# A quarter of the second pass's raw weights loaded early, no loads in ScalarE's queue, and the last rotations in another order

## The chip, the cores and the metric

The kernel runs on one core of a Trainium2 chip. A core has TensorE (PE in the profile; its weight loads are PEld), VectorE (DVE), ScalarE (ACT), GpSimd (POOL) and SyncE (SP), and 16 DMA engines that move data between HBM and the core. SP, ACT and POOL can issue transfers; the profile writes SPq, ACTq and POOLq for that. Each engine works through its own list of instructions in order and waits for others by semaphores. The metric is the device time of one execution in microseconds (us); a kernel's time is the median of its runs.

## The reference, cut to what matters

One decoder layer on x of 4096 tokens by 1024, in float32: an RMSNorm, one projection into eight parts, dilated softmax attention (8 heads of 64, three branches), retention (4 heads, key width 64, value width 128) in chunks of 128 tokens, SiLU gates, an output projection, the residual and a last RMSNorm.

```python
h = rms_norm(x, norm_gain[layer])
proj = h @ w_in
qa, ka, va, ga, qr, kr, vr, gr = jnp.split(proj, cuts, axis=-1)
attn = merge_heads(dilated_attention(split_heads(qa, 8), split_heads(ka, 8), split_heads(va, 8)))
ret = merge_heads(retention(split_heads(qr, 4), split_heads(kr, 4), split_heads(vr, 4)))
mixed = jnp.concatenate([jax.nn.silu(ga) * attn, jax.nn.silu(gr) * ret * ret_gn_gain], axis=-1)
x = x + mixed @ w_out
return rms_norm(x, final_gain)
```

q and k of attention are rotated by position in halves of 32, q and k of retention in pairs. All of the output is needed to float32 precision.

## The kernel before

**Products.** Each float32 factor is split in a high part, rounded on ACT to the type that PE takes (fp32r), and a low part, the difference, on DVE or POOL; a product is three matmuls (hi hi, hi lo, lo hi).

**Phase 1** (function `phase1`) makes q, k, v and the retention's q and k from `w1`, in two passes over the tokens: pass 0 makes k of attention and v, pass 1 q of attention and q and k of retention. Each pass has 8 blocks of 512 tokens. A block is done by a scheme with seven products of half the size (P1, P5, P6, P3, P7, P2, P4, in this order) instead of eight; each product takes two steps (one for each bank of output columns), so a block has 14 steps (`STEPS`) of 48/2 = 24 matmuls. The products' right sides are quarters of the weights (A and B are the two halves of the raw rows of `w1`; rows 0 to 511 are "a", rows 512 to 1023 "b") or sums of them: D = A - B of "a" on POOL, S1, S2 and S4 on DVE. Each is split before use, and all splits together need more room than there is: `HOMES` names, for each product and pass, the tiles that its hi and lo parts lie in, and `ROOM` what tiles these are (most belong to phase 2: wh, w0 to w7, q00 to q11, hr, hc, kk; p40 and p41 are phase 1's own). So at the change of passes the raw weights of pass 1 (4 MB) come into tiles that pass 0 has done with, are scaled, summed and split there, and the splits go into tiles that later products of pass 0 free: P1 of pass 1 goes to kk, which P3 of pass 0 holds up to its last matmul.

**The order** is written by hand. The loop at the end of `phase1` goes through the steps; `at(step, fn, ...)` lists what is issued behind a step's matmuls, with front=True ahead of what is listed already. `s = STEPS * NBLK` is the first step of pass 1 and `STEPS * NB2` the end of the phase. A step says where an instruction stands in its engine's list, not when it runs. For block q, `hi_x` and `lo_x` split x (tile h), `snapshot` (ACT) and `join` (DVE) carry sums over between PSUM banks (tile m), `values` (ACT) and `store_values` write v, `rotate` (DVE, six operations on 128x512) turns q and k, `hi_o`/`lo_o` split what was turned (tile hl) and `store_o`, `store_r` store it. For the norm, tokens are loaded as rows into the tiles "xn" and "tabR" (`load_n`) and squared on ACT (`square`); pass 1 uses "tabR" for the rotation's tables and "xn" for parts of P4's weights, loaded a second time (`split_p4`, tile `raw`).

**Phase 2** is attention and retention. Its instructions are built from two generators: `attention` (score products S into two PSUM banks, row maximum on DVE, exponential P on ACT, transposes T, products with v) and `filler` (chunk after chunk of 128 tokens: values V of retention with weights `w2`, in 8 steps k, with `scores` Rs, `decayed_q` qg, `decayed_k` kd, `outputs` Ro, `next_state`, of the chunk before). Filler runs alone up to `LEAD`, and then as the slots of attention allow. Each chunk's x is loaded as hr (one tile) and split into hc (three tiles). Its first loads are issued in phase 1 (`first_k`, `first_q`, `first_chunk`) or at its start (`first_loads`): the constants and the mask on SP, and the rest of head 0's q (columns 512 to 2047) and k (from 1024) by ACT. **Phase 3** makes the gates and the output projection.

## Time and profile before

| what | value |
|---|---|
| runs | 2404.93, 2403.29, 2402.48 us, median 2403.29 |
| profiled execution | 2404.88 us, span 2403.1 us |
| PE busy | 2276.7 us, 95% of the span |
| DVE, ACT, POOL busy | 1736.7, 1140.5, 785.3 us |
| DMA | 405.07 MB, mean 169 GB/s |
| granted TensorE clock, mean | 0.98 |

The span is the time from the first to the last instruction of the profiled execution; the execution's own time lies 1.8 us above it. Times of rows are in us from the span's start. The page cuts the span in 40 slices of 60 us and gives the busy share of each in tenths:

```profile
PE   6999995999994999999999999998899999999998
```

PE is at 9 almost everywhere; the first slice, the seventh (360 to 420, the change of passes), the thirteenth (720 to 780, from phase 1 to phase 2) and two around 1700 (phase 2 to 3) lie below. A row of a timeline gives start, length, engine, line, operation, what it writes and reads, how often; in brackets stands how long the engine had been idle and what ended that.

### The profile page before, as it was taken

The numbers are of one execution on the slowest core, as the hardware profiler recorded it, in microseconds if no ns is written. First come the engines' busy times: TensorE is split into PE (matmuls) and PEld (weight loads), VectorE is DVE, ScalarE is ACT, GpSimd is POOL, SyncE is SP. The second block draws the span as 40 slices with busy tenths as digits, with TensorE's granted clock in tenths as the row PEclk, the third lists the DMA queues.
The fourth block names the chain that finished last, engine by engine and source line by source line (L and its number), as shares of the span: only waits on it lengthen the run. The fifth ranks groups of instructions, "written<-read, shape, count | busy, mean of one in ns | idle before, by whom it ended". The sixth has DMA issues, their size and how long they took to land. (4 is left out here: it accounts for less than half of the span.)

```text
span 2403.1 us, 47344 instructions
## 1 busy us (share of the span) xinstructions
PE 2276.7 (95%) x16808; PEld 2049.9 (85%) x16808; DVE 1736.7 (72%) x4231; ACT 1140.5 (47%) x3082; POOL 785.3 (33%) x961
## 2 busy tenths in 40 slices
PE   6999995999994999999999999998899999999998
PEld 5899995999993888888888888877789999999997
DVE  6776867998985878787887879786665655655654
ACT  5555554332331666767666666667322322322221
POOL 1343433222222545344543535456121121121110
PEclk8999998999997999999999999999999999999999
DMA  6678775555468565758585775746676665566653
GB/s 193 202 235 273 225 239 174 175 152 180 151 190 198 134 160 140 186 124 194 136 179 144 160 159 133 177 129 194 147 184 156 144 170 152 141 164 154 148 154 92
DMA packets 447789, 405.07 MB, mean 169 GB/s; under 512 B 210040, under 2 KB 397176, under 8 KB 442688
## 3 DMA queue, kind: packets, MB, share of 16 engines
q1 hardware_dynamic: 412112, 324.79, 52.9%
q0 software_dynamic: 29968, 57.07, 8.0%
q10 hardware_dynamic: 5472, 20.19, 2.6%
q8 instruction: 133, 2.18, 0.4%
q14 instruction: 104, 0.85, 0.1%
HBM read 283.12 MB, written 118.64 MB: 167 GB/s over the span
## 5 line engine op out<-in xcount | busy, mean ns | idle before, releaser
L1064 DVE CUSTOM_DVE_ANT_0 S<-S,mask 128x256 f32<-128x256 f32 (+1 forms) x768 | 308.6, 402 | 165.2 <-PE S L1043 127.3
L1071 ACT ACTIVATE P<-S,nm 128x256 f32<-128x256 f32 (+1 forms) x768 | 337.3, 449 | 46.5 <-DVE nm L1064 43.4
L50 PE MATMUL g<-h,wg 128*128 128x256 f32 x1024 | 289.4, 283 | 0.0
L323 ACT ACTIVATE h<-xt 128x1024 fp32r<-128x1024 f32 (+1 forms) x115 | 119.5, 1039 | 246.8 <-DVE xt L315 105.8
L1080 PE MATMUL T<-ident,P 128*128 128x128 f32 x1368 | 213.6, 274 | 0.0
L49 PE MATMUL po<-wo,m 128*128 128x512 f32 x512 | 200.8, 392 | 0.1
L1632 POOL TENSOR_TENSOR rs<-v,mhalf 128x1 f32<-128x1 f32 x32 | 17.5, 547 | 547.2 <-DVE v L1630 529.0
L50 PEld LDWEIGHTS g<-h,wg 128*128 128x128 f32 x1024 | 195.8, 191 | 0.0
L1113 PE MATMUL O<-pt,v 128*64 128x128 f32 (+1 forms) x1968 | 195.7, 325 | 0.0
L1043 PE MATMUL S<-kk,qc 128*128 128x256 f32 x1024 | 187.2, 306 | 7.0 <-issue 2.7
L48 PE MATMUL po<-wohi,m 128*128 128x512 f32 x448 | 178.7, 399 | 7.7 <-ACT m L40 6.6
L1043 PEld LDWEIGHTS S<-kk,qc 128*128 128x128 f32 x1024 | 149.8, 190 | 35.6 <-issue 17.1
L50 PE MATMUL po<-wohi,m 128*128 128x512 f32 x448 | 177.7, 397 | 0.2 <-DVE m L41 0.2
L811 POOL TENSOR_TENSOR hc<-hr,hc 128x512 fp32r<-128x512 f32 x64 | 86.4, 1351 | 266.8 <-ACT hc L810 196.5
L1113 PEld LDWEIGHTS O<-pt,v 128*64 128x64 f32 x1968 | 121.1, 137 | 60.4 <-issue 31.5
L1080 PEld LDWEIGHTS T<-ident,P 128*128 128x128 f32 x1368 | 164.1, 141 | 0.2 <-ACT wg0hi L87 0.2
L327 DVE TENSOR_TENSOR h<-xt,h 128x1024 fp32r<-128x1024 f32 (+1 forms) x115 | 137.8, 1198 | 36.5 <-ACT h L323 36.4
L1571 ACT ACTIVATE e<-g 128x256 f32<-128x256 f32 x128 | 48.3, 379 | 239.2 <-PE g L50 222.8
L40 ACT ACTIVATE m<-e 128x256 fp32r<-128x256 f32 x128 | 53.1, 417 | 227.8 <-DVE e L1578 133.7
L1071 ACT ACTIVATION_READ_ACCUMULATOR P<-S,nm 128x1 f32 x768 | 157.6, 205 | 0.0
L48 PE MATMUL g<-h,wg1hi 128*128 128x256 f32 x512 | 144.8, 284 | 2.3 <-ACT e L1571 2.3
L49 PE MATMUL g<-h,wg1hi 128*128 128x256 f32 x512 | 145.8, 285 | 1.1 <-DVE h L859 0.9
(278 smaller groups left out, 6519.2 us busy)
## 6 DMA issues: line engine op xcount, KB each, us to landing
hr<-in_xT_dram SPq DMA_DIRECT2D x61, 512.0 KB
xt<-in_xT_dram POOLq DMA_DIRECT2D x60, 512.0 KB, 9.1
q<-dr_q SPq DMA_DIRECT2D x120, 256.0 KB
v<-dr_v SPq DMA_DIRECT2D x96, 256.0 KB
wb<-dr_w SPq DMA_DIRECT2D x128, 192.0 KB
o<-dr_o SPq DMA_DIRECT2D x192, 128.0 KB
xn<-in_x_dram ACTq DMA_DIRECT2D x32, 512.0 KB
dr_v<-vo SPq DMA_DIRECT2D x64, 256.0 KB
```

Source lines behind the costliest of these rows:

```text
L40: nc.scalar.activation(dst[:, 0], src, AF.Copy)
L48: nc.tensor.matmul(out, wh, xh, start=first and i == 0, stop=False)
L49: nc.tensor.matmul(out, wh, xl, start=False, stop=False)
L50: nc.tensor.matmul(out, wl, xh, start=False, stop=last and i == n - 1)
L323: nc.scalar.activation(xs[q, prod][:, 0, ks, :], xq[(q, *SOURCE[prod])][:, ks, :], AF.Copy)
L327: (engine or nc.vector).tensor_tensor(h[:, 1, ks, :], src[:, ks, :], f32(h[:, 0, ks, :]), ALU.subtract)
L811: nc.gpsimd.tensor_tensor(hc[:, :, 1, :], src, hc[:, :, 0, :].bitcast(F32), ALU.subtract)
L1043: nc.tensor.matmul(s[:, j * 256 : (j + 1) * 256], qq[h, t, half][:, off : off + 128] if br == 0 else it["q"][:, t, i, :], rhs, start=(j == ...
L1064: nc.vector.tensor_tensor_reduce(sv, sv, mask[:, it["br"], c0:256], 1.0, BIG, ALU.add, ALU.min, accum_out=nm[:, col : col + 1])
L1071: nc.scalar.activation(it["P", i // 2][:, i % 2, c0:256], sv, AF.Exp, bias=nm[:, col : col + 1], scale=-1.0, accum_out=den[:, col : col + 1])
L1080: nc.tensor.transpose(t[:, j * 128 : (j + 1) * 128], it["P", bank][:, j // 2, j % 2 * 128 : j % 2 * 128 + 128], ident)
L1113: nc.tensor.matmul(o[64 * bank : 64 * bank + 64, c0 : c0 + 128 * m], vt[h, br, idx // 8][:, idx % 8, :], it["pt"][:, a : a + m, :].rearran ...
```

## The change

Five things change together.

1. *Raw weights of pass 1.* A `Raw` no longer names its rooms when it is made; `load` takes tiles one after the other and loads all rows that a tile holds in two transfers (one for each range of columns), where there were two for each row block of 128. Rows 0 of "a" go into tile "tabR" at step s - 17, rows 1 into "xn" at s - 14 (each half a MB), rows 2 and 3 of "a" into wh0 and rows 0 and 1 of "b" into wh1 at s - 13, and the last two of "b" into p40 at s - 11. Before, "a" went into wh0 and wh1 at s - 12, and "b" into p40 and q01 at s - 10 and s - 8.
2. *Splits and sums of pass 1.* P1's split stands ahead of the scaling of B of "b" and of S1; S1, S2, S4 and the splits of P5 and P6 move one or two steps later; P2's split comes before P7's. P2 now lies in q01 and q11, P4 in p40 and q00.
3. *First loads of phase 2.* The rest of head 0's k is loaded by POOL at the 5th step before the end of phase 1, all of q's first half by SP behind the last step; ACT issues none. The constants and the mask stand on SP behind all stores of phase 1.
4. *The last block.* The second rotation of retention's parts, which stood right after attention's first, is the last of all; for attention's second half the hi parts are made by DVE, ahead of the lo parts, and the stores come sooner.
5. *The first chunks of phase 2.* The first half of chunk 1 is split in phase 1; for chunk 1, `scores`, `decayed_q`, `decayed_k` and the first `outputs` stand at later steps k. At the kernel's start, the raw weights of pass 0 for rows 2 and 3, and those of "b", come in fewer, larger transfers, too.

DVE at the change of passes, before, from the last joins of z (line 428) in block 7. In the names, w1kk is P1's home, w1wh, w1p and w1q hold raw weights, h is a split of x, m a sum carried over, t and o the rotation:

```order
L428 TENSOR_TENSOR m_4010<-z_3833,m_4010 128x512
L428 TENSOR_TENSOR m_4045<-z_3880,m_4045 128x512
L275 SCALAR_TENSOR_TENSOR w1kk<-w1wh_3858,gain_all,w1kk 128x512 x2
L275 SCALAR_TENSOR_TENSOR w1kk<-w1wh_3859,gain_all,w1kk 128x512 x2
L280 SCALAR_TENSOR_TENSOR w1wh_3858<-w1wh_3858,gain_all,w1p_3934 128x4x128 x2
L280 SCALAR_TENSOR_TENSOR w1wh_3859<-w1wh_3859,gain_all,w1q_3935 128x4x128 x2
L327 TENSOR_TENSOR h_4071<-xt_3378,h_4071 128x1024
L428 TENSOR_TENSOR m_3975<-x_3755,m_3975 128x512
L280 SCALAR_TENSOR_TENSOR w1p_3934<-w1q_4014,gain_all,w1p_3934 128x4x128 x2
L280 SCALAR_TENSOR_TENSOR w1q_3935<-w1q_4014,gain_all,w1q_3935 128x4x128 x2
L428 TENSOR_TENSOR m_3977<-x_3791,m_3977 128x512
```

The same place in the change (lines are some 5 higher; raw is weights in the tiles tabR and xn):

```order
L433 TENSOR_TENSOR m_3999<-z_3839,m_3999 128x512
L433 TENSOR_TENSOR m_4034<-z_3876,m_4034 128x512
L280 SCALAR_TENSOR_TENSOR w1kk<-raw_3663,gain_all,w1kk 128x512
L280 SCALAR_TENSOR_TENSOR w1kk<-raw_3788,gain_all,w1kk 128x512
L280 SCALAR_TENSOR_TENSOR w1kk<-w1wh_3816,gain_all,w1kk 128x512 x2
L332 TENSOR_TENSOR h_4060<-xt_3372,h_4060 128x1024
L433 TENSOR_TENSOR m_3968<-x_3752,m_3968 128x512
L433 TENSOR_TENSOR m_3970<-x_3791,m_3970 128x512
L484 TENSOR_TENSOR t_1_4132<-m_3968,tab_3749 128x512
```

The sums S1 and S2 (L280 in the first list) have left the stretch; both joins of x stand directly behind P1's split and one h.

ACT from the end of phase 1, before: hl is the split of the rotated q, hc that of a chunk, vch the values of chunk 0:

```order
L916 DMA q_00_8130<-dr_q 32x1536 x3
L509 ACTIVATE hl_8126<-o_1_8046 128x512
L509 ACTIVATE hl_8127<-o_1_8047 128x512
L810 ACTIVATE hc_8140<-hr_7979 128x4x128
L810 ACTIVATE hc_8143<-hr_7979 128x4x128
L916 DMA q_00_8130<-dr_q 32x1536
L916 DMA q_10_8135<-dr_q 32x1536 x3
L509 ACTIVATE hl_8199<-o_1_8174 128x512
L509 ACTIVATE hl_8200<-o_1_8175 128x512
L916 DMA q_10_8135<-dr_q 32x1536
L821 DMA kk_7759<-dr_k 32x3072 x4
L810 ACTIVATE hc_8358<-hr_8146 128x4x128
```

and in the change:

```order
L516 ACTIVATE hl_8111<-o_1_8039 128x512
L516 ACTIVATE hl_8112<-o_1_8040 128x512
L831 ACTIVATE hc_8115<-hr_7968 128x4x128
L831 ACTIVATE hc_8118<-hr_7968 128x4x128
L831 ACTIVATE hc_8186<-hr_8121 128x4x128
L1434 ACTIVATE vch_8356<-V_8331,rs_all 128x512
L831 ACTIVATE hc_8362<-hr_8121 128x4x128
```

Twelve loads and two hl have left ACT's list; chunk 0, chunk 1 and vch stand next to each other.

SP over the same place, in the change (before, the constants from L955 stood ahead of the last sixteen stores, and the loads of 32x1536 on ACT):

```order
L937 DMA q_00_8158<-dr_q 32x512 x4
L937 DMA q_10_8163<-dr_q 32x512 x4
L532 DMA dr_q<-hl_8111 128x2x256 x2
L532 DMA dr_q<-hl_8112 128x2x256 x2
L937 DMA q_00_8158<-dr_q 32x1536 x4
L937 DMA q_10_8163<-dr_q 32x1536 x4
L498 DMA dr_r<-or_8172 4x32x256 x4
L532 DMA dr_q<-hl_8180 128x2x256 x2
L532 DMA dr_q<-hl_8181 128x2x256 x2
L498 DMA dr_r<-or_8197 4x32x256 x4
L976 DMA decay_8296<-in_decayT_dram 128x512
```

Behind the last row come the three small constants, the mask and the first two loads of v.

The diff, without blank lines:

```diff
@@ -217,8 +217,8 @@
                 "P6": ("h1", "q10"),
                 "P3": ("h0", "p41"),
                 "P7": ("wh0", "wh1"),
-                "P2": ("q00", "q11"),
-                "P4": ("p40", "q01"),
+                "P2": ("q01", "q11"),
+                "P4": ("p40", "q00"),
             },
         )
@@ -231,15 +231,20 @@
         class Raw:
-            def __init__(self, ps, rooms, k0):
-                self.ps, self.k0 = ps, k0
...
-
-            def load(self, k):
-                for i, c0 in enumerate(COLS[self.ps]):
-                    nc.sync.dma_start(self.tiles[k][:, i, :], io["w1"][(self.k0 + k) * 128 : (self.k0 + k + 1) * 128, c0 : c0 + 512])
+            def __init__(self, ps, k0):
+                self.ps, self.k0, self.A, self.B = ps, k0, [], []
+
+            def load(self, *tiles):
+
+                for t in tiles:
+                    r0, n = (self.k0 + len(self.A)) * 128, t.shape[1] // 2
+                    for i, c0 in enumerate(COLS[self.ps]):
+                        src = io["w1"][r0 : r0 + n * 128, c0 : c0 + 512].rearrange("(k p) c -> p k c", p=128)
+                        nc.sync.dma_start(t.rearrange("p (k i) c -> p i k c", i=2)[:, i], src)
+                    for k in range(n):
...
         def load_b(ps, dst, k):
@@ -501,11 +506,13 @@
...
-        def hi_o(q, half):
+        def hi_o(q, half, on_vector=False):
             hls[q, half] = [hlp.tile([128, 2, BLK], F32R, tag="hl", name="hl1") for _ in range(2)]
             for hl, o in zip(hls[q, half], turned[q, 0, half]):
                 hi, _, src = parts_of(q, hl, o)
-                if q >= NBLK:
+                if on_vector:
+                    nc.vector.tensor_scalar(hi, src, -0.125, None, ALU.mult)
+                elif q >= NBLK:
                     nc.scalar.activation(hi, src, AF.Copy, scale=-0.125)
                 else:
                     nc.scalar.activation(hi, src, AF.Copy)
@@ -597,9 +604,10 @@
             at(s + 13, lo_o, q, 1)
             at(s + 13, rotate, q, 0, 0)
             at(s + 14, store_o, q, 1)
-            at(s + 16, hi_o, q, 0)
-            at(s + 18, lo_o, q, 0)
-            at(s + 19, store_o, q, 0)
+            last = q == NB2 - 1
+            at(s + (15 if last else 16), hi_o, q, 0, last)
+            at(s + (15 if last else 18), lo_o, q, 0)
+            at(s + (17 if last else 19), store_o, q, 0)
             if one:
...
                 at(s + 15, store_values, q, 0)
             else:
                 end = q == NB2 - 1
-                at(s + 15, rotate, q, 1, 0)
-                at(s + (11 if end else 17), rotate, q, 1, 1)
-                at(s + 17, store_r, q, 0)
-                at(s + (14 if end else 18), store_r, q, 1)
+                at(s + (14 if end else 15), rotate, q, 1, 0)
+                at(s + (16 if end else 17), rotate, q, 1, 1)
+                at(s + (16 if end else 17), store_r, q, 0)
+                at(s + 18, store_r, q, 1)
         raw = {}
...
+        raw["a"], raw["b"] = Raw(1, 0), Raw(1, 4)
+        raw["Aa"], raw["Ba"], raw["Ab"], raw["Bb"] = raw["a"].A, raw["a"].B, raw["b"].A, raw["b"].B
+
+        def load_raw(name, room):
+            if room in ROOM:
+                raw[name].load(*ROOM[room](F32).tiles)
+            else:
+                raw[name].load(tp.tile([128, 2, 512], F32, tag=room, name="raw1"))
         def diff_d():
...
         s = STEPS * NBLK
-        at(s - 12, load_raw, "a", range(4), front=True)
-        at(s - 12, open_raw, "a", ("wh0", "wh1"), 0, front=True)
-        at(s - 10, load_raw, "b", (0, 1), front=True)
-        at(s - 10, open_raw, "b", ("p40", "q01"), 4, front=True)
-        at(s - 8, load_raw, "b", (2, 3), front=True)
+
+        at(s - 17, load_raw, "a", "tabR")
+        at(s - 14, load_raw, "a", "xn")
+        at(s - 13, load_raw, "b", "wh1", front=True)
+        at(s - 13, load_raw, "a", "wh0", front=True)
+        at(s - 11, load_raw, "b", "p40", front=True)
         at(s - 8, diff_d)
-        at(s - 6, lambda: scale_b(raw["Bb"]))
         at(s - 6, split, 1, "P1", "Aa", 0)
-        at(s - 6, sum_s1)
-        at(s - 5, sum_s2)
-        at(s - 4, split, 1, "P5", "Ba")
-        at(s - 3, sum_s4)
-        at(s - 2, split, 1, "P6", "Bb")
+        at(s - 5, lambda: scale_b(raw["Bb"]))
+        at(s - 4, sum_s1)
+        at(s - 3, sum_s2)
+        at(s - 3, split, 1, "P5", "Ba")
+        at(s - 2, sum_s4)
+        at(s - 1, split, 1, "P6", "Bb")
         at(s + 1, split, 1, "P3", "Aa")
-        at(s + 3, split, 1, "P7", "D", 0)
-        at(s + 5, split, 1, "P2", "Ab", 1)
+        at(s + 3, split, 1, "P2", "Ab", 1)
+        at(s + 5, split, 1, "P7", "D", 0)
...
@@ -690,14 +700,21 @@
         def first_k():
             ahead["kk"] = load_k(nc, kka, dr, 0, nc.gpsimd.dma_start, slice(0, 1024))
-        def first_q():
-            ahead["qq"] = {(0, i, 0): load_q(nc, qp, dr, 0, i, 0, None, slice(0, 512)) for i in range(2)}
+        def rest_k():
+            load_k(nc, kka, dr, 0, nc.gpsimd.dma_start, slice(1024, S), ahead["kk"])
+
+        def first_q(i0, i1):
+            cols = slice(i0, i1)
+            ahead["qq"] = {(0, i, 0): load_q(nc, qp, dr, 0, i, 0, None, cols, ahead.get("qq", {}).get((0, i, 0))) for i in range(2)}
...
+        def second_chunk_split():
+            ahead["hch"][1].append(split_h_chunk(nc, hcp, ahead["hr"], 1, 0))
+
         def first_chunk_split():
-            ahead["hch"] = {0: [split_h_chunk(nc, hcp, raw["hr"], 0, j) for j in range(2)]}
+            ahead["hch"] = {0: [split_h_chunk(nc, hcp, raw["hr"], 0, j) for j in range(2)], 1: []}
             ahead["hr"] = load_x_chunk(nc, hcp, io, 1, nc.gpsimd.dma_start)
         s = STEPS * NB2
@@ -707,18 +724,22 @@
         for i in range(2):
             at(s - 4 + i, w2_split, range(4 * i, 4 * i + 4), front=True)
         at(s - 6, first_chunk)
-        at(s - 2, first_q)
+        at(s - 5, rest_k)
+        at(s, first_q, 0, 512, front=True)
+        at(s + 2, first_q, 512, S // 2, front=True)
+        at(s + 1, second_chunk_split)
         at(s - 2, first_chunk_split)
-        X, Y = Raw(0, ("h1", "q10"), 0), Raw(0, ("q11", "p41"), 4)
+        X, Y = Raw(0, 0), Raw(0, 4)
         Aa, Ba, Ab, Bb = X.A, X.B, Y.A, Y.B
-        for k in range(4):
-            X.load(k)
-            load_x(0, 0, 0, k)
+        first = [t for r in ("h1", "q10") for t in ROOM[r](F32).tiles]
+        for i, t in enumerate(first):
+            X.load(t)
+            for k in ((0,), (1,), (2, 3))[i]:
+                load_x(0, 0, 0, k)
         load_x(0, 0, 1)
-        for k in range(4):
-            Y.load(k)
+        Y.load(*(t for r in ("q11", "p41") for t in ROOM[r](F32).tiles))
         for half in (1, 0):
             load_x(0, 1, half)
...
@@ -1291,9 +1312,6 @@
         def first_loads():
             load_constants()
-            for i in range(2):
-                load_q(nc, qp, dr, 0, i, 0, nc.scalar.dma_start, slice(512, S // 2), qq[0, i, 0])
-            load_k(nc, kka, dr, 0, nc.scalar.dma_start, slice(1024, S), kk[0])
...
                     yield 648 if c < NCH else 0
-                    if mid and k == 1:
+
+                    if mid and k == (6 if c == 1 else 1):
                         scores(mid)
                         decayed_q(mid)
                         yield 654
-                    if mid and k == 3:
+                    if mid and k == (7 if c == 1 else 3):
                         decayed_k(mid)
                         yield 2 * TRN
...
                     if k == HL and 1 <= c < NCH - 1:
                         hraw[c + 1] = load_x_chunk(nc, hcp, io, c + 1, nc.gpsimd.dma_start if c < 3 else None)
-                    if k == HS and c < NCH - 1:
+                    if k == HS and c + 1 not in hch and c < NCH - 1:
...
                     if k == 6:
-                        if mid:
+                        if mid and c > 1:
                             outputs(mid, 0)
                             yield 872
                         if old:
                             ret_out(c - 2, old)
                             yield 4 * TRN
                 if mid:
+                    if c == 1:
+                        outputs(mid, 0)
+                        yield 872
                     outputs(mid, 1)
                     yield 872
                     next_state(mid)
```

More of the change, by code (lines that the diff above doesn't have):

```diff
@@ L231, in phase1 @@
         class Raw:
-            def __init__(self, ps, rooms, k0):
-                self.ps, self.k0 = ps, k0
-                self.tiles = [t[:, i : i + 2, :] for r in rooms for t in ROOM[r](F32).tiles for i in range(0, t.shape[1], 2)]
-                both = [t.rearrange("p q (u t c) -> p (q u) t c", t=2, c=128) for t in self.tiles]
-                self.A, self.B = ([t[:, :, i, :] for t in both] for i in range(2))
-            def load(self, k):
-                for i, c0 in enumerate(COLS[self.ps]):
-                    nc.sync.dma_start(self.tiles[k][:, i, :], io["w1"][(self.k0 + k) * 128 : (self.k0 + k + 1) * 128, c0 : c0 + 512])
+            def __init__(self, ps, k0):
[7 more added lines that the diff above has]
+                    for k in range(n):
+                        both = t[:, 2 * k : 2 * k + 2, :].rearrange("p q (u t c) -> p (q u) t c", t=2, c=128)
+                        self.A.append(both[:, :, 0, :])
+                        self.B.append(both[:, :, 1, :])
         def load_b(ps, dst, k):
@@ L609, in phase1 @@
                 end = q == NB2 - 1
-                at(s + 15, rotate, q, 1, 0)
-                at(s + (11 if end else 17), rotate, q, 1, 1)
-                at(s + 17, store_r, q, 0)
-                at(s + (14 if end else 18), store_r, q, 1)
+                at(s + (14 if end else 15), rotate, q, 1, 0)
+                at(s + (16 if end else 17), rotate, q, 1, 1)
+                at(s + (16 if end else 17), store_r, q, 0)
+                at(s + 18, store_r, q, 1)
         raw = {}
-        def open_raw(name, rooms, k0):
-            raw[name] = Raw(1, rooms, k0)
-            raw["A" + name], raw["B" + name] = raw[name].A, raw[name].B
-        def load_raw(name, ks):
-            for k in ks:
-                raw[name].load(k)
+        raw["a"], raw["b"] = Raw(1, 0), Raw(1, 4)
[5 more added lines that the diff above has]
+                raw[name].load(tp.tile([128, 2, 512], F32, tag=room, name="raw1"))
         def diff_d():
```

## The prediction

> **What bounds the kernel now.** I read the slices of the page first, then windows around the slices in which TensorE is not busy, then the timelines of the engines there. Windows of the kernel before (stretch, length, busy us of PE, PEld, DVE, ACT, POOL with their counts, granted clock, DMA share, GB/s):
>
> ```profile
> 360.00:380.00 20.00, 8.96 (x76) 8.76 (x74) 3.06 (x5) 6.28 (x9) 5.85 (x5) 0.79 0.67 226
> 380.00:400.00 20.00, 12.51 (x72) 12.13 (x72) 19.93 (x30) 9.86 (x16) 6.34 (x11) 0.70 0.35 102
> 400.00:420.00 20.00, 14.07 (x103) 13.86 (x104) 18.85 (x25) 10.87 (x19) 9.01 (x15) 0.91 0.70 199
> 430.60:728.50 297.90, 297.90 (x2496) 297.90 (x2496) 269.97 (x367) 95.89 (x132) 66.35 (x96) 1.00 0.55 166
> 740.00:760.00 20.00, 0.00 (x0) 0.00 (x0) 7.96 (x16) 2.44 (x5) 2.54 (x4) 0.50 0.70 203
> 760.00:780.00 20.00, 12.79 (x59) 10.94 (x60) 3.77 (x15) 3.46 (x12) 5.61 (x6) 0.76 1.03 186
> 780.00:1650.00 870.00, 856.85 (x6718) 718.46 (x6718) 697.30 (x2556) 596.24 (x2049) 407.31 (x459) 1.00 0.65 154
> ```
>
> Between 430.6 and 728.5 PE is busy all the time, and from 780 on nearly so. So PE is the bound, and what is won in the two holes (the change of weights, 360 to 431, and the start of phase 2, 729 to 778) goes through to the end one for one. All terms below are starts of PE work that come earlier.
>
> **The first hole.** Rows of the timelines (start, length, engine, line, operation; in brackets the idle time before it and what ended it):
>
> ```profile
> 354.50 3.01 PE L415 MATMUL z<-w1kk,h 128*128 128x256 f32 x24
> 357.55 1.06 ACT L323 ACTIVATE h<-xt 128x1024 fp32r<-128x1024 f32 x1 [3.69 <-PE z L415]
> 374.27 0.72 ACT L288 ACTIVATE w1q<-w1q,gain_all 128x512 f32<-128x512 f32 x1 [4.83 <-DMA w1q<-in_w_dram]
> 376.20 2.54 ACT L274 ACTIVATE w1kk<-w1wh,gain_all 128x512 fp32r<-128x512 f32 x4
> 376.94 2.74 DVE L275 SCALAR_TENSOR_TENSOR w1kk<-w1wh,gain_all,w1kk 128x512 fp32r<-128x512 f32 x4 [18.55 <-ACT w1kk L274]
> 376.94:409.15 32.21, 15.78 (x97) 15.19 (x97) 32.10 (x46) 13.98 (x23) 12.74 (x22) 0.76 0.38 113
> 384.21 0.77 PE L415 MATMUL x<-h,w1q 128*128 128x256 f32 x2 [15.25 <-DVE m L428]
> 409.20 7.35 PE L415 MATMUL z<-h,w1w 128*128 128x256 f32 x47 [4.51 <-DVE h L327]
> 410.12 6.21 SPq L249 DMA_DIRECT2D raw<-in_w_dram  x4
> 428.40 0.72 ACT L274 ACTIVATE w1p<-raw,gain_all 128x512 fp32r<-128x512 f32 x1 [1.10 <-DMA raw<-in_w_dram]
> 430.60 6.02 PE L415 MATMUL x<-h,w1wh 128*128 128x256 f32 x48 [2.63 <-ACT m L423]
> ```
>
> PE waits for a join on DVE, DVE for ACT's first half of P1's split (w1kk), and ACT stands before it at four scalings of raw weights, the last of which land at 374.27 and later. From 376.94 DVE is busy 32.10 of 32.21 us, up to the h that releases P5 at 409.20: once released, DVE's own work paces PE.
>
> What the change does there: ACT splits P1 before it scales, on rows 0 to 3 that lie in the two early tiles and the first tile to be loaded late; DVE does P1's rest, one h and both joins, and only then the sums. P1's destination w1kk is read by PE until 357.51. So ACT: h to 358.6, first w1kk 0.64 more, 359.25; DVE starts at **359.3** instead of 376.94, 17.6 earlier. Behind that come, up to the h of P5, the same 46 instructions as now, in another order, 32.2 us: P5 starts at 391.5 and not at 409.20. The joins that PE waited 15.25 for stand some 5 us into this run (P1's 2.74, one h, two joins) and end near 364.5, before PE gets to them at 384.21 - 15.25 = 368.96. P1's second half still waits for ACT's values, which stand behind the sums (4 us by my count of the rows); that hides in the wait for P5. Swapping P2 and P7 moves equal work.
>
> Do the bytes allow it? What DMA carried there:
>
> ```profile
> 339.00:375.00 36.00, 29.96 (x252) 29.76 (x251) 11.56 (x12) 12.29 (x16) 14.23 (x19) 0.95 0.89 282
> ```
>
> 10.2 MB (36 us at 282) from 339 to the last landings at 374 and 375, at 0.89 of the engines' time. Of these, half a MB now comes at 325, and some 1.5 MB (one x tile, four k stores) falls behind the last weights instead of before them. 8.1 MB at 282 GB/s end at 368. P1's own part is the first 1.5 MB of these and has landed by 355 even with two others' MB among it; the last quarter (p40) is wanted by DVE's third sum at 369.6, less 1.4 for ACT's scaling: 368. It just fits. If the rate stays, 0; if they land as late as today (375.5) DVE waits some 8 us, and the gain is 9.
>
> The repeated load for P4 now goes into a tile that P3's split frees at about 396. It released ACT at 428.40 today and through it PE at 430.60. Shifted by 17.6 it must land by 410.8. Four loads issued from 396 on, over some 6 us as today's were, have 9 to 15 us to land; today's, issued from 410.12, took up to 18. Up to 3 lost. I take **17.0** for this hole (bounds 9 and 18).
>
> **The second hole.** Rows (ACTq is ACT's own issuing of loads), and two rows of the list of DMA issues between 700 and 800, whose last number is the median us to landing:
>
> ```profile
> 731.33 9.66 ACTq L916 DMA_DIRECT2D q<-dr_q  x3
> 750.48 8.29 ACTq L821 DMA_DIRECT2D kk<-dr_k  x4
> 758.82 0.63 ACT L810 ACTIVATE hc<-hr 128x512 fp32r<-128x512 f32 x1 [14.67 <-DMA dr_q<-hl]
> 760.08 0.80 PE L48 MATMUL V<-w2hi,hc 128*128 128x512 f32 x1 [23.69 <-ACT vch L1416]
> 759.58 2.50 POOL L811 TENSOR_TENSOR hc<-hr,hc 128x512 fp32r<-128x512 f32 x2 [9.29 <-issue]
> 762.04 1.52 POOL L1316 TENSOR_TENSOR qg<-rq,qdec 64x256 f32<-64x256 f32 x2
> 763.50 0.93 POOL L799 DMA_DIRECT2D hr<-in_xT_dram  x1
> 776.14 0.63 ACT L810 ACTIVATE hc<-hr 128x512 fp32r<-128x512 f32 x1 [15.61 <-DMA hr<-in_xT_dram]
> 777.63 1.22 PE L1043 MATMUL S<-kk,q 128*128 128x256 f32 x4 [7.13 <-ACT P L1071]
> 745.56 1.29 DVE L517 SCALAR_TENSOR_TENSOR hl<-o,hl 128x512 fp32r<-128x512 f32 x2
> 747.72 0.29 DVE L1283 CAST rkh<-rk 128x256 fp32r<-128x256 f32 x1
> 748.78 1.51 POOL L1287 TENSOR_TENSOR qbd<-rq,qbd 64x256 fp32r<-64x256 f32 x2
> 706.04 7.23 SPq L493 DMA_DIRECT2D dr_r<-or  x4
> 737.05 2.74 SPq L525 DMA_DIRECT2D dr_q<-hl  x4
> 739.83 9.58 SPq L493 DMA_DIRECT2D dr_r<-or  x8
> 753.85 3.42 SPq L992 DMA_DIRECT2D v<-dr_v  x2
> hr<-in_xT_dram POOLq DMA_DIRECT2D x3, 512.0 KB, 5.8
> rq<-dr_r POOLq DMA_DIRECT2D x1, 128.0 KB, 5.4
> ```
>
> ACT is held in its own queue by eight q and four k loads until 758.8. Behind them stand chunk 1's hc and vch, PE's V (760.08), POOL's hc, the load of chunk 2 (763.50), and its landing at 776.14, which gates the exponentials and PE's third score product at 777.63.
>
> Without the loads ACT is free at 729, and the next to be late is DVE. Its last rotations, splits and casts are the same set plus two hi on DVE; I take those like the L517 rows, 0.65 each: rkh ends at 748.0 + 1.3 = 749.3. POOL: rkl 0.7, qbd 1.5, then, by the new order, the second half of chunk 1, 1.25: 752.8. Only then can POOL issue chunk 2: **10.7 earlier** than 763.50. Its landing took 12.6 here, the median is 5.8; I take 9, 762.7.
>
> SP pays. The constants and the mask, issued by 732 today, now stand behind everything: 36 DMAs ahead of the mask from 728.9 on (q00 is read by the last product now, so the first q loads cannot go at 723). SP's 18 issues from 737.05 to 757.27 came 1.12 apart, while ACT issued some nine more: 0.75 apart for both. At 0.85 the mask goes at 759.5 and lands at 762.5. Bounds: 0.75 gives 759, 1.12 gives 772.
>
> With both there at 762.7: ACT 0.6, POOL's half 1.25, qg 1.5, the output products under 1, then the third score product at 766.9: 10.7 earlier than 777.63. One thing is given back: DVE now takes chunk 1's rq before the third row maximum, and that load cannot go until qg is done (766.0); with 3 to 5.4 to land, 0 to 2 lost, I take 0.7. **10.0** for this hole, bounds 1 (mask at 772) and 15 (chunk 2 in 5.8 and no loss).
>
> The Trainium skill speaks against part of this: "DMA: Bandwidth & Descriptors", section "Rules for kernel authors", says that spreading DMAs over SP, ACT and GpSimd does not help bandwidth, since all run on the same 16 engines. By that, the boundary is set by bytes: about 7.1 MB from 728.9 to the mask and chunk 2, at the 186 to 203 GB/s of the windows above, end at 764 to 767, and the term would be 6 to 9.
>
> The k loads on POOL cost nothing: POOL stands idle 13.6 us before its first hc, and they land long before the first score product.
>
> ```profile
> 729.77 2.97 POOL L811 TENSOR_TENSOR hc<-hr,hc 128x512 fp32r<-128x512 f32 x2 [13.61 <-ACT hc L810]
> ```
>
> **The start.** Rows 2 and 3 of the first weights come as one pair of loads, so row 2 waits for row 3:
>
> ```profile
> 12.78 0.72 ACT L274 ACTIVATE w1wh<-w1q,gain_all 128x512 fp32r<-128x512 f32 x1 [1.04 <-DMA w1q<-in_w_dram]
> 14.56 0.72 ACT L274 ACTIVATE w1wh<-w1q,gain_all 128x512 fp32r<-128x512 f32 x1 [0.76 <-DMA w1q<-in_w_dram]
> ```
>
> Between 0 (fewer issues) and 1.8 lost; I take **0.7**.
>
> Sum: 17.0 + 10.0 - 0.7 = 26.3 off the span of 2403.1. The profiled execution took 2404.88, 1.8 around its span and 1.6 over the median of 2403.29; against the median it is **2377.0**.
>
> **Rivals.** (1) SP's queue paces the boundary at its 1.12: mask at 772, the second term about 1, 2386. For it: dr_r x8 above is 1.2 each. Against: ACT's loads took turns with them. (2) The raw weights land as late as now, because DMA is at 0.89 there: the first term is 9, 2385. Against: they are issued some 6 us earlier. (3) Both holes close altogether, as if only loads were missing: 27 idle in the first (11.0 + 7.5 + 5.9 + 2.6 by the windows and the row at 430.60) and 31 in the second (23.69 + 7.13), 2403 - 58 = 2345. Against: DVE's 32.1 of 32.2. (4) Slower: the same mask. If each of the 36 issues takes over 1.6 us, it lands at 790, the third score product comes 16 us later than now, and the first hole's gain is gone; at 1.7 it is about 2406. Four dr_r stores at 706 took 1.8 each, but waited for data. (5) It does not do what it says: an early tile frees late, SP stands at it, and stores and weights move back together: 2403.
>
> **Chances.** Forecast 0.58 (own range 2370 to 2384), rival (1) 0.15, (2) 0.13, (3) 0.04, (4) 0.06, (5) 0.04. The range 2366 to 2391 holds the forecast, (1) and (2) with their unknown costs and leaves (3) to (5) out. A difference of 0.2% (4.8 us) is about what can be told from none. Faster 0.90, within 0.04, slower 0.06.
>
> **What would show it.** In the trace after: DVE's first w1kk row at 359 to 360; P5's first product 15 to 18 earlier than 409.20; no 23.69 before V, a wait for POOL's hc instead near 745 to 753; chunk 2's load issued by POOL near 753; the third score product at 764 to 770. I am wrong if DVE waits for p40's scaling after 368, if the first row maximum waits for the mask past 770, or if PE idles again between 413 and 729.

## The result

The changed kernel took 2383.28 us, the kernel before 2404.11 (medians of four runs each); the ratio is 0.991 with a 95% interval of 0.989 to 0.9931, so 17 to 26 us faster. The forecast was 2377.0 with a range of 2366 to 2391. The profiled execution has a span of 2382.8 us against 2403.1.

The windows of the changed kernel that answer to those shown of before (columns as there):

```profile
345.00:360.00 15.00, 15.00 (x128) 15.00 (x127) 9.43 (x9) 6.43 (x10) 11.20 (x11) 1.00 1.03 335
360.00:380.00 20.00, 18.52 (x156) 18.32 (x154) 19.67 (x29) 14.40 (x24) 5.98 (x12) 1.00 0.68 227
380.00:400.00 20.00, 13.33 (x67) 13.04 (x68) 18.85 (x26) 7.96 (x13) 8.35 (x14) 0.66 0.71 217
400.00:420.00 20.00, 20.00 (x170) 20.00 (x169) 18.00 (x24) 14.15 (x22) 3.77 (x5) 1.00 0.70 207
431.00:700.00 269.00, 267.39 (x2235) 266.61 (x2234) 241.79 (x327) 84.21 (x115) 64.78 (x94) 1.00 0.57 168
700.00:740.00 40.00, 25.23 (x144) 21.74 (x143) 32.30 (x55) 9.27 (x15) 9.77 (x12) 0.79 0.78 207
740.00:760.00 20.00, 9.79 (x52) 8.87 (x51) 4.74 (x18) 3.69 (x13) 4.88 (x7) 0.75 0.66 185
780.00:1650.00 870.00, 853.52 (x6703) 717.32 (x6702) 690.29 (x2510) 596.86 (x2032) 406.90 (x460) 1.00 0.66 156
```

DVE's work (the third busy column) now fills 360 to 380, where it had 3.06 us, and PE's first stretch without work has shrunk to 1.5 us there and 6.7 in the next 20. At the start of phase 2, PE still stands for 25 of the 60 us from 700 to 760.

**The first hole**, rows of the changed kernel's timelines:

```profile
360.26 1.41 DVE L280 SCALAR_TENSOR_TENSOR w1kk<-raw,gain_all,w1kk 128x512 fp32r<-128x512 f32 x2 [0.87 <-ACT w1kk L279]
368.71 1.34 ACT L293 ACTIVATE w1p<-w1p,gain_all 128x512 f32<-128x512 f32 x2 [5.42 <-DMA w1p<-in_w_dram]
382.09 5.49 PE L420 MATMUL x<-h,w1kk 128*128 128x256 f32 x24 [3.56 <-ACT vo L445]
392.37 7.90 PE L420 MATMUL z<-h,w1w 128*128 128x256 f32 x42 [4.58 <-DVE h L332]
412.61 2.56 SPq L254 DMA_DIRECT2D raw<-in_w_dram  x4
417.15 0.75 DVE L280 SCALAR_TENSOR_TENSOR w1q<-raw,gain_all,w1p 128x512 fp32r<-128x512 f32 x1 [1.02 <-ACT w1p L279]
418.79 0.75 DVE L280 SCALAR_TENSOR_TENSOR w1q<-raw,gain_all,w1p 128x512 fp32r<-128x512 f32 x1 [0.89 <-ACT w1p L279]
443.18 0.39 PE L420 MATMUL x<-h,w1hc 128*128 128x256 f32 x1 [1.24 <-DVE h L332]
```

DVE's first w1kk row runs at 360.26 (376.94 before) and P5 goes on at 392.37 (409.20 before). The 15.25 us for a join is gone. What is new is a wait of 1.24 at 443, where PE did not stand before. Between 360 and there DVE pauses three times, for 1.05 us at 395.76 and twice for the second half of P4's repeated weights (the two rows of DVE's L280 at 417 and 418), and from 419.45 on not at all.

**The second hole**, rows of SP's, DVE's, PE's and POOL's timelines:

```profile
688.17 2.02 POOL L842 DMA_DIRECT2D kk<-dr_k  x4
690.12 17.25 SPq L498 DMA_DIRECT2D dr_r<-or  x4
707.28 0.73 ACT L83 ACTIVATE w2hi<-raw,gain_all 128x512 fp32r<-128x512 f32 x1 [1.62 <-DMA raw<-in_w_dram]
722.16 0.79 PE L48 MATMUL V<-w2hi,hc 128*128 128x512 f32 x1 [9.41 <-ACT hc L831]
724.43 4.50 SPq L937 DMA_DIRECT2D q<-dr_q  x8
747.37 0.43 SPq L976 DMA_DIRECT2D mask<-in_masks_dram  x1
753.43 0.30 DVE L1085 CUSTOM_DVE_ANT_0 S<-S,mask 128x128 f32<-128x128 f32 x1 [19.45 <-DMA mask<-in_masks_dram]
754.91 0.69 PE L1339 MATMUL Rk<-ident,rk 128*128 128x128 f32 x2 [10.21 <-DVE stm L1329]
```

Phase 1 now ends at 712.75 and not at 728.77. The waits of 23.69 and 7.13 have gone, and three others stand there: 9.41 for chunk 0, 5.22 for vch, and 10.21 for DVE, which waits for the mask.

### The profile page after: what moved, and what is told of

Read it like the earlier page. It is cut to its first block, busy times and chain, and to the rows that moved or that the text cites. A ratio compares the mean times of both kernels' runs of the same rounds, so it can differ in the third digit from the quotient of the medians.

```text
span 2382.8 us, 47338 instructions
## 1 busy us (share of the span) xinstructions
PE 2282.6 (96%) x16808; PEld 2055.8 (86%) x16808; DVE 1736.4 (73%) x4233; ACT 1138.4 (48%) x3080; POOL 786.5 (33%) x965
## 5 line engine op out<-in xcount | busy, mean ns | idle before, releaser
L1085 DVE CUSTOM_DVE_ANT_0 S<-S,mask 128x256 f32<-128x256 f32 (+1 forms) x768 | 308.6, 402 | 173.3 <-PE S L1064 119.6
```

Of the source, the lines that this page charges most:

```text
L1085: nc.vector.tensor_tensor_reduce(sv, sv, mask[:, it["br"], c0:256], 1.0, BIG, ALU.add, ALU.min, accum_out=nm[:, col : col + 1])
```

## The experiments

One profile of a kernel differs from the next by some us in places that no edit touches, so beside each median three stretches are given, read from PE's and DVE's rows: the start (where PE's products of P7 with w1w begin after their wait, near 59), the change of passes (from the first row of y behind 300, P2 of block 6, to the end of phase 1's last product) and the boundary (from there to the fourth kd on DVE). "Against" is the ratio to the kernel before on the same chip, with its 95% interval; the kernel before took 2405.69, 2406.01, 2407.69 and 2408.64 us beside the four groups of runs, so ratios tell more than medians from group to group (order_only to bound_only and const_pool are one group; dve_more, p6_pool, chunk0_pool and both_pool the second; the next three the third).

| kernel | median us | against before | start | change of passes | boundary |
|---|---|---|---|---|---|
| before | 2404.11 | | 58.69 | 406.65 | 121.4 |
| changed | 2383.28 | 0.991 (0.989 to 0.9931) | 60.52 | 389.47 | 116.6 |
| order_only | 2393.66 | 0.9941 (0.9921 to 0.9961) | 59.29 | 395.28 | 122.1 |
| loads_old_order | 2393.14 | 0.9947 (0.9927 to 0.9966) | 60.71 | 400.48 | 117.0 |
| bound_only | 2402.46 | 0.9982 (0.9968 to 0.9996) | 59.18 | 404.75 | 117.4 |
| dve_more | 2394.12 | 0.9958 (0.9938 to 0.9979) | 61.12 | 395.60 | 117.6 |
| p6_pool | 2386.40 | 0.9916 (0.9893 to 0.994) | 60.19 | 392.13 | 115.0 |
| const_pool | 2390.69 | 0.9921 (0.9892 to 0.9949) | 59.92 | 392.57 | 118.1 |
| chunk0_pool | 2383.26 | 0.991 (0.989 to 0.9931) | 60.90 | 388.68 | 113.5 |
| both_pool | 2389.79 | 0.9931 (0.9913 to 0.995) | 59.78 | 389.37 | 115.9 |
| three_chains | 2385.77 | 0.9908 (0.9889 to 0.9927) | 60.74 | 392.07 | 117.6 |
| three_chains_single | 2386.25 | 0.991 (0.9891 to 0.993) | 58.54 | 389.07 | 119.6 |
| after_again (changed) | 2385.15 | 0.9902 (0.9883 to 0.9922) | 59.75 | 392.11 | 114.7 |
| more_bytes | 2391.93 | 0.9925 (0.9906 to 0.9943) | 60.79 | 390.23 | 121.9 |

Eight kernels have the changed kernel's code at the change of passes without an edit: 388.7 to 392.6. Most of this scatter is one wait: DVE's pauses for the second half of P4's repeated weights add up to between 0.5 us (chunk0_pool) and 4.1 us (three_chains), 1.9 in the changed kernel's first profile, and with them taken off the eight lie at 387.6 to 388.7. At the boundary the changed kernel read 116.6 and 114.7.

### The change of passes: order, loads, or DVE

**order_only** puts the order alone into the kernel before:

```diff
-        at(s - 6, lambda: scale_b(raw["Bb"]))
         at(s - 6, split, 1, "P1", "Aa", 0)
-        at(s - 6, sum_s1)
-        at(s - 5, sum_s2)
-        at(s - 4, split, 1, "P5", "Ba")
-        at(s - 3, sum_s4)
-        at(s - 2, split, 1, "P6", "Bb")
+        at(s - 5, lambda: scale_b(raw["Bb"]))
+        at(s - 4, sum_s1)
+        at(s - 3, sum_s2)
+        at(s - 3, split, 1, "P5", "Ba")
+        at(s - 2, sum_s4)
+        at(s - 1, split, 1, "P6", "Bb")
```

> The kernel before, with one edit: at the change of passes P1's split stands ahead of the scaling of the raw weights on ACT, and the sums come later in DVE's list; loads and tiles as before. Theory (DVE's own list paces PE from the first w1kk row on, and the order decides when that row can run): raw rows of 'a' have landed by about 364, so DVE starts near 365 instead of 376.94, has about 10 us of work that needs no scaled row, and stalls 1 to 2 us for the rows that land at 374 to 375: about 10 us faster, 2394. Rival (the quarter that comes early is what wins, the order alone is nothing): 2403 to 2404, with P5's first product still near 409.

**loads_old_order** is the opposite: the changed kernel with these lines as they were before.

> The changed kernel, with one edit: at the change of passes ACT scales the four raw rows first and DVE makes the sums S1 and S2 right behind P1's split, in the order of before; the early tiles and all loads as changed. Theory (DVE's list paces): ACT stands at the last raw rows, which were scaled at 368.71, so the first w1kk row on DVE moves from 360.3 to about 370.7: some 10 us slower than the changed kernel, 2393. Rival (the loads win, the order is nothing): as the changed kernel, 2383.

Rows of order_only, then of loads_old_order:

```profile
361.63 1.17 DVE L275 SCALAR_TENSOR_TENSOR w1kk<-w1wh,gain_all,w1kk 128x512 fp32r<-128x512 f32 x1 [1.06 <-ACT w1kk L274]
366.75 3.20 DVE L275 SCALAR_TENSOR_TENSOR w1kk<-w1wh,gain_all,w1kk 128x512 fp32r<-128x512 f32 x2 [0.21 <-ACT w1kk L274]
377.48 0.72 ACT L288 ACTIVATE w1q<-w1q,gain_all 128x512 f32<-128x512 f32 x1 [2.28 <-DMA w1q<-in_w_dram]
```

```profile
372.93 1.33 ACT L293 ACTIVATE w1p<-w1p,gain_all 128x512 f32<-128x512 f32 x2 [6.30 <-DMA w1p<-in_w_dram]
374.90 1.41 DVE L280 SCALAR_TENSOR_TENSOR w1kk<-raw,gain_all,w1kk 128x512 fp32r<-128x512 f32 x2 [10.93 <-ACT w1kk L279]
```

With the order alone, DVE works on P1 while the last raw rows are still landing (377.48): the stretch is 11.4 us shorter, the kernel faster by 0.6%. Without the order, the early quarter has landed and is not used: DVE stands 10.93 us for ACT, the stretch is 11.0 us longer than the changed kernel's. The theory's 10 and 10.4 hold; the rival falls twice. The loads have a share of their own: they take the stretch from order_only's 395.3 to the 388.7 to 392.6 of the changed code, and without the order from the 404.8 and 406.7 of the old code to 400.5. The new homes of P2 and P4 and their order changed with the loads; no run separates them.

**dve_more** repeats DVE's subtractions of P3's split, which changes no value:

```diff
-                    (engine or nc.vector).tensor_tensor(lo, src[k], f32(hi), ALU.subtract)
+                    for _ in range(3 if (ps, prod) == (1, "P3") else 1):
+                        (engine or nc.vector).tensor_tensor(lo, src[k], f32(hi), ALU.subtract)
```

> The changed kernel, with DVE's four subtractions of P3's split (128x512, 0.65 us each) done three times over at the change of passes: 8 instructions, 5.2 us of DVE work that nothing needs, behind the h that releases P5. Theory (DVE is saturated from the first w1kk row to the h that PE waits for at 443, so every us of its list there is a us of the kernel): the end of phase 1 and the kernel 4 to 5 us later, 2388. Rival (past P5's start, near 392, PE or the loads pace, and DVE catches up by itself): within 1 us of the changed kernel.

Rows of dve_more (lines are one higher):

```profile
398.88 4.20 DVE L278 TENSOR_TENSOR w1p<-raw,w1hr 128x512 fp32r<-128x512 f32 x6 [1.05 <-ACT w1hr L276]
408.38 0.58 PE L421 MATMUL x<-h,w1hc 128*128 128x256 f32 x1 [5.65 <-DVE h L333]
```

The added work, 5.8 us (4.20 and 4.19 us instead of twice 1.29), stands as a wait of 5.65 before PE and stays: the stretch is 6.1 us longer than in the changed kernel's first profile, of which 0.5 lies ahead of the edit. DVE paces PE there; it does not catch up. By the medians the kernel is 4 to 11 us slower than the three that ran beside it.

**p6_pool** gives four of DVE's subtractions to POOL:

```diff
-        at(s - 1, split, 1, "P6", "Bb")
+        at(s - 1, split, 1, "P6", "Bb", None, nc.gpsimd)
```

> The changed kernel, with the four subtractions of P6's split moved from DVE to POOL, which idles there. Theory (DVE's list paces): DVE is 2.6 us lighter, P5 starts 2.4 us earlier and the kernel is 2 to 2.6 us faster, 2381. Rival (POOL's 128x512 operations hold DVE up: an h of 1.22 us took 2.31 while POOL made D at 355.9): what DVE is spared it loses again, within 1 us, or slower by up to 2.

POOL's and DVE's rows of p6_pool:

```profile
381.65 2.51 POOL L277 TENSOR_TENSOR w1q<-w1wh,w1hc 128x512 fp32r<-128x512 f32 x2
384.11 2.51 POOL L277 TENSOR_TENSOR w1q<-w1p,w1hc 128x512 fp32r<-128x512 f32 x2
380.37 6.82 DVE L285 SCALAR_TENSOR_TENSOR raw<-w1wh,gain_all 128x512 f32<-128x512 f32 x2
395.40 4.83 PE L420 MATMUL z<-h,w1w 128*128 128x256 f32 x27 [7.50 <-DVE h L332]
```

The two DVE operations that took 1.41 us in the changed kernel took 6.82: DVE stood for as long as POOL's four ran, 381.65 to 386.62. PE's wait ahead of P5 is 7.50 and not 4.58. The rival holds, and more than it said: DVE loses 5.4 us and is spared 2.5. The stretch of 392.13 lies inside the scatter, but DVE's pauses for P4's weights are only 0.5 us in it; with them taken off it is 391.6, 3 to 4 us more than in the eight kernels. No gain is seen in the median.

### The boundary: what ends it

**bound_only** is the kernel before with the parts of the change at the start of phase 2 alone (the ScalarE loads, the last rotations, POOL's k loads, the constants behind the stores and chunk 1's scores).

> The kernel before, with only the parts of the change at the start of phase 2: no loads in ACT's queue, the order of the last rotations, constants and mask behind the last stores, POOL's k loads, and where chunk 1's scores stand. Theory (SP's queue sets the mask, and with it the first row maximum): worth 4 to 6 us, 2398 to 2400, with the row maximum waiting for the mask some 40 us after the last product of phase 1. Rival (the 4.7 us that this place gave in the changed kernel are small only because the weights part made SP and the landings late there): the 10 us of the forecast, 2393.

The boundary is 4.0 us shorter than before and the kernel 0.2% faster (3.2 us by the medians beside each other, 1 to 8 by the interval): the low end of the theory's 4 to 6. The rival (this part gives 10 where the weights don't disturb it) falls.

**const_pool** takes the mask and the constants off SP's queue:

```diff
-            for t, n in ((decay, "decayT"), (qdec, "qdec"), (kdec, "kdec"), (cdec, "cdec"), (mask, "masks")):
-                nc.sync.dma_start(t, io[n])
+            for t, n in ((mask, "masks"), (decay, "decayT"), (qdec, "qdec"), (kdec, "kdec"), (cdec, "cdec")):
+                nc.gpsimd.dma_start(t, io[n])
```

> The changed kernel, with one edit: the mask and the four constants are loaded by POOL, mask first, instead of by SP behind 36 issues. Theory (the mask is what ends the wait at the boundary: DVE stood 19.45 us for it up to 753.43, and PE 10.21 behind that): POOL issues it near 727, it lands before 740, and what comes next is chunk 2's hc at 748.2, so the third score product moves from 757 to about 749.5: 7 to 8 us faster than the changed kernel, 2375 to 2377. Rival (bytes set the boundary, whoever issues): the same bytes must land, at most 2 us faster, 2381 to 2383.

```profile
731.25 0.56 POOL L976 DMA_DIRECT2D mask<-in_masks_dram  x1
748.17 0.30 DVE L1085 CUSTOM_DVE_ANT_0 S<-S,mask 128x128 f32<-128x128 f32 x1 [9.35 <-PE S L1064]
763.00 0.61 DVE L1303 CAST qbd<-rq 64x256 fp32r<-64x256 f32 x2 [10.83 <-DMA rq<-dr_r]
```

The mask is no longer waited for, and nothing is won: DVE now stands 10.83 us for chunk 1's q (rq), which the changed kernel's row maximum stood ahead of. My theory's 7 to 8 us fell; only the wait was right. The rival, at most 2 us faster, stands.

**chunk0_pool** loads chunk 0's x from POOL, **both_pool** does both:

```diff
-            raw["hr"] = load_x_chunk(nc, hcp, io, 0)
+            raw["hr"] = load_x_chunk(nc, hcp, io, 0, nc.gpsimd.dma_start)
```

> The changed kernel, with chunk 0's x loaded by POOL as soon as P3's last product frees its tile, instead of by SP behind the stores of block 14. Theory (two chains end together at the boundary: the mask behind SP's 36 issues, and the chunks, each loaded when the one before is split, with chunk 1's q behind them): PE's wait before the first V, 9.41, goes, and the chunks come some 8 us earlier, but the mask still lands near 753: 0 to 3 us faster, 2380 to 2383. Rival (the chunks alone set the end): 7 to 9 us faster, 2375.

> Chunk 0's x and the mask with the constants both loaded by POOL. Theory of two chains that end together: only now does the boundary become shorter, by 6 to 9 us against the changed kernel, 2375 to 2377; what ends it then are DVE's last rotations and chunk 1's q. Rival (bytes: the same 7 MB have to land): within 2 us of the changed kernel.

SP's and POOL's rows of chunk0_pool, and DVE's and PE's of both_pool:

```profile
692.37 6.30 SPq L498 DMA_DIRECT2D dr_r<-or  x4
698.78 14.99 SPq L532 DMA_DIRECT2D dr_q<-hl  x4
698.15 1.99 POOL L842 DMA_DIRECT2D kk<-dr_k  x4
```

```profile
743.38 0.30 DVE L1085 CUSTOM_DVE_ANT_0 S<-S,mask 128x128 f32<-128x128 f32 x1 [5.37 <-PE S L1064]
753.24 0.80 PE L1355 MATMUL Ro<-state,qg 128*128 128x128 f32 x2 [5.08 <-POOL qg L1334]
760.51 0.61 DVE L1303 CAST qbd<-rq 64x256 fp32r<-64x256 f32 x2 [11.82 <-DMA rq<-dr_r]
```

chunk0_pool: PE's wait ahead of the first V falls from 9.41 to 3.17 and the boundary by 3.1 or 1.2 (against the two profiles of the changed kernel), as expected, and the kernel's time is the same. both_pool: the first row maximum runs 25.8 us after phase 1's end (40.7 in the changed kernel), and the fourth kd comes no earlier: 11.82 us for rq, whose load SP issues behind all its stores and after POOL's qg. The theory of two chains fell too.

**three_chains** adds, to both_pool, POOL's qg ahead of chunk 2's hc and the split of chunk 1's q and k behind the state on DVE; **three_chains_single** also loads the first weights' rows 2 and 3 one by one.

```diff
+                    if mid and c == 1 and k == HL:
+                        decayed_q(mid)
...
-                    if k == 7 and 1 <= c < NCH:
+                    if k == 7 and 2 <= c < NCH:
                         split_rk(res[c])
...
                     next_state(mid)
+                    if c == 1:
+                        split_rk(res[c])
```

> Chunk 0's x and the mask with the constants by POOL, as in the run before, and beside that: on POOL the decayed q (qg) of chunk 0 stands ahead of chunk 2's hc, and on DVE the split of chunk 1's q and k stands behind the state, not ahead of the third row maximum. Theory (three waits of nearly one length lie behind each other at the boundary: the mask, the chunks, and chunk 1's q, whose load waits for qg and goes through SP's queue; each one taken away alone shows the next): DVE's 11.82 and PE's 5.08 of the run before go, the fourth kd comes 6 to 9 us earlier after the end of phase 1 than in the changed kernel (116.6 there), 108 to 111, and the kernel is 2375 to 2378 against 2384 for the changed one. Rival (bytes: 7 MB have to land whoever issues and whatever waits): the fourth kd at 114 to 117, no gain.

> The kernel of the run beside it, and the first weights' rows 2 and 3 loaded one by one again, as in the kernel before the change. Theory (row 2 waits for row 3's transfer): 1 to 1.8 us faster than the run beside it, seen as the third row's first scaling on ACT near 13 instead of 14.98. Rival (more issues cost what the row wins): no difference.

> The changed kernel itself, beside the two others: 2383 to 2386 by both theories; it tells how far one profile of the same kernel lies from another.

Rows of three_chains:

```profile
749.94 1.22 PE L1064 MATMUL S<-kk,q 128*128 128x256 f32 x4 [3.94 <-ACT P L1092]
754.60 4.15 SPq L997 DMA_DIRECT2D q<-dr_q  x8
768.01 2.07 DVE L1040 CAST qc<-q 128x512 fp32r<-128x512 f32 x1 [3.86 <-DMA v<-dr_v]
772.27 1.20 PE L1064 MATMUL S<-kk,qc 128*128 128x256 f32 x4 [5.38 <-ACT P L1092]
```

The third score product starts 35.4 us after phase 1's end instead of 44.2, and 22 us later PE stands 5.38 us before a product of qc, the q of the spread branches. DVE's cast of qc had stood 3.86 us for a load: it reads the q whose last eight loads SP issued from 754.60 on, and the profile names the load of v behind them; which of the two came last isn't settled. The fourth kd is at 117.6: no gain, the rival's figure. The single rows are scaled earlier, as the theory had it (the third at 12.79 instead of 15.06), and PE's start is at 58.54 against 60.74; in the median nothing of it is seen.

**more_bytes** asks whether bytes or SP's issuing pace this: one transfer more on POOL, read by nobody.

```diff
+            "spare": [768, BLK],
...
+            nc.gpsimd.dma_start(dr["spare"], dr["q"].rearrange("i t h d s -> (i t h d) s")[0:768, 6 * BLK : 7 * BLK])
             load_constants()
```

> The changed kernel, and at the end of phase 1 POOL issues one more transfer: 1.57 MB of stored q copied to a place in memory that nobody reads. Theory (at the boundary bytes set the pace: whatever is last in line lands when all before it has): 1.57 MB at the 200 GB/s of this place are 7.9 us, SP's issues and the mask behind them come later by it, and the fourth kd moves from 115 to 117 us behind the end of phase 1 to 122 to 125. Rival (SP's own issuing sets the pace, at 0.8 us for each of 36, and the DMA engines have room): SP's queue and the mask as they are, the fourth kd within 2 us.

```profile
730.33 9.60 SPq L937 DMA_DIRECT2D q<-dr_q  x8
756.71 0.43 SPq L976 DMA_DIRECT2D mask<-in_masks_dram  x1
```

The eight q loads behind it took SP 9.60 us to issue, 4.50 in the changed kernel; the mask was there 44.8 us after phase 1's end instead of 40.7, and the boundary is 5.3 and 7.2 us longer than in the two profiles of the changed kernel. The list of SP's waits says why: for landings of earlier stores and loads of q it stood 7.2 us ahead of q loads there (4.6 and 2.6), 1.1 in the changed kernel. SP goes on as earlier transfers land, so its pace is itself a matter of bytes: the theory, with two thirds to nine tenths of its 7.9 us. The fourth kd, at 121.9, just misses the theory's 122 to 125. This is one profile; the intervals of the ratios, 0.9925 against 0.991 and 0.9902, overlap.

## Why the prediction was right, and where its sizes were off

**What bounds the kernel, and the first hole (17.0): right, by its own reason.** In the first profile the stretch is 17.2 us shorter. Over the eight profiles of this code (mean 390.4) and the two of the old code (405.7) it is 15.3, inside the bounds of 9 and 18. DVE's start was said at 359.3 and came at 360.26; P5 was said at 391.5 and came at 392.37, 16.83 earlier. The bytes just fitted, as the prediction had them: the last raw rows were scaled at 368.71, said 368, and DVE did not stand for them.

What was sized too small is the repeated load for P4 ("up to 3 lost"; the sum took 0.6, 17.6 to 17.0). It comes in two halves through one tile, and the prediction weighed the first alone. The first, issued at 397.09, was scaled at 407.40, in time. The second can go only when DVE has read the first: it was issued at 412.61 and scaled at 416.39 and 418.03, and DVE stood 1.02 and 0.89 us for it. PE did not wait there, but paid later: it waits 1.24 us for DVE's h at 443.18, and the same in all eight profiles of this code, so up to there DVE still paces PE. From P5's start to that wait it is 49.3 us where DVE's pauses for P4 add up to 0.5, and 53.0 where they add up to 4.1; the mean of the pauses is 2.2. From the wait to the end of phase 1 it is 269.6 in all eight. The gain is DVE's earlier start, less what DVE loses on the way. By the prediction's own words PE idle between 413 and 729 was a sign of being wrong; it came, 1.24 us at 443.18 and 0.35 at 435.92, as a matter of size.

**The second hole (10.0): the right wait, half the size.** The first profile gives 4.8 us. The mean boundary of six profiles of the changed code there (changed, after_again, loads_old_order, bound_only, dve_more, p6_pool) is 116.4, that of the two with the old 121.8: 5.4. Two steps were off.

The first is the mask's landing. It was said to land 33.7 us after phase 1's end (762.5 less 728.8) and was waited for until 40.7. Of the 7.0, 3.5 are SP's late start: its first q load went 3.5 us after phase 1's end and not with it, because stores ahead of it took 17.25 us for four issues and the load of chunk 0's x and a small one stood behind these.

The sentence of the prediction that was wrong is that the k loads on POOL cost nothing. They went out at 688.17, the last w2 weights, issued just behind, were used at 707.28, and SP stood in between. From 690 to 707 the DMA engines were busy 0.95 of the time and moved 175 GB/s; at the same place of the kernel before (706 to 723) it was 0.79 and 213 GB/s. In the two profiles without k loads there (before, order_only) SP's eight stores behind the w2 weights took 10.7 and 11.2 us, in the twelve with them 21.3 to 22.6. In chunk0_pool the k loads went ten us later, at 698.15, and the stall moved to the next four stores (14.99); in the kernel before, the four stores at 706.04 took 7.23. But the 3.5 us are not what the k loads cost: in chunk0_pool SP's first q load does go with phase 1's end (0.07 us behind it), and the mask is waited for until 38.4, only 2.3 and 1.0 us less than in the two profiles of the changed kernel.

Another 3.1 of the 7.0 are the landing (6.1 us after the issue at 747.37, not 3.0). The pace itself was right: 31.1 us for the issues in between against 30.6. The third score product follows the mask by 3.5 us, said 4.4, so it comes 44.2 us after phase 1's end and not 38.1.

The second is that an earlier third score product was passed on one for one. In the changed kernel this holds: from it to the fourth kd it is 72.4 us, 72.6 before. It ends where the product comes still earlier. In const_pool, both_pool, three_chains and three_chains_single it starts 34.9 to 40.5 us after phase 1's end, 77.6 to 84.7 us lie behind it, and the boundary is 115.9 to 119.6. The forecast's 38.1 lies among these, so by these runs a mask on time would have given about 2 to 6 us and not 10. Behind the mask stood more than the prediction had: chunk 1's q, and then the last loads of head 0's q and of v. The runs that took one of these waits away each showed the next.

The prediction's signs for this hole are in the times of the kernel before; phase 1 now ends 16.0 us earlier. With these added, chunk 2's load was issued at 755.7 (said near 753), the first row maximum waited for the mask until 769.5 (wrong past 770, so only just not), and the third score product started at 773.0, outside 764 to 770.

The rule that was weighed there, the Trainium skill's "DMA: Bandwidth & Descriptors", section "Rules for kernel authors" (spreading transfers over issuing engines gives no bandwidth), agrees with the runs: const_pool, both_pool and three_chains moved loads from SP to POOL and won nothing (ratios 0.9921, 0.9931 and 0.9908, 0.991 and 0.9902 for the changed kernel). By that rule the term was to be 6 to 9; measured is 4.8 to 5.4. That more bytes cost time is more_bytes' own result: its boundary is 5 to 7 us longer.

**The start (-0.7): too small.** Of 14 profiles, the four with single rows begin P7's products at 58.5 to 59.3, the ten with the pair at 59.8 to 61.1: 1.5 us lost by the means, inside the bounds of 0 and 1.8.

**The sum.** 15.3 + 5.4 - 1.5 = 19.2, against 20.8 between the medians; forecast 26.3. Rival (1), the mask at 772 by SP's pace of 1.12 us, is nearer in the number (2386 is 2.7 us away, the forecast 6.3) and in when the mask came (769.5 in before's time), but not by its reason: SP's pace was 0.86 (31.1 us for 36 issues), and the term is 4.8 to 5.4 and not its 1. That its sum comes out close is in part luck, since the first hole and the start gave less than both had. Rival (2), late weights, and rival (3), both holes closed, are ruled out by DVE's rows; (4) and (5) by the issues' 0.86 us and by the tiles that came free in time. The 9.41 us ahead of the first V were in no case.

What stays open: no run had the k loads in another engine's queue or at another time with all else equal, so their part in the stall is read from where it goes, and what they cost the kernel isn't known. Nor did a run move P4's second half, or settle what ends the boundary once mask, chunks and rq are early. None of the experiments beat the changed kernel beyond its uncertainty.

## What to carry to other kernels

When one engine's queue is full from the moment it is released (here DVE, 32.10 of 32.21 us), the gain of a change is the earlier start of that queue, and putting first what needs no late data can be worth more than the earlier data (here 11.4 us for the order alone, 4.3 to 6.2 for the loads alone). What such an engine waits for on the way is lost to the kernel too, even where PE does not stand at that moment. Where a boundary is a bundle of loads, removing the wait that ends last shows the next one of nearly the same length; ask first how many bytes have to land before the last consumer can go. A load that is hidden for its own reader can still delay the stores and loads behind it: look at who issues next.

## What was not expected of the hardware

While POOL ran four subtractions of 128x512 (two inputs each, 5.0 us), a pair of DVE operations with two inputs each took 6.82 us and not 1.41. The first of the pair took its 0.74 us, the second 6.16: it ended at 387.18, 0.56 behind POOL's last. The Trainium skill's "SBUF — State Buffer", section "SBUF: two separate sides", says that the two engines share a port pair as an exclusive lock that is held for the whole instruction; the trace agrees in that DVE stood while POOL's four, 1.27 to 1.28 us each, took their usual time. It isn't always all four: in the changed kernel at 355.88 an h of DVE beside POOL's subtractions for D took 2.31 us and not 1.22 and ended ahead of POOL's last one, and POOL's last two took 1.74 and 2.28 us and not 1.29. What decides between the two is open. So POOL's idle time was no place for DVE's work here, although DVE was the bound.

What SP needs for a group of issues is not a constant: eight q loads of one form took 4.50 us, and 9.60 with 1.57 MB more under way, most of it waits for landings between issues of 0.30 to 0.66. In the 17.25 us above, one store's issue alone took 9.74.
